# Logits of the second attention branch: two heads on the two halves of the array's rows

## The chip, the core and the metric

The kernel runs on one core of a Trainium2 chip. The metric is the device time of one execution in microseconds (us), the median of several runs. TensorE (PE below) multiplies matrices: it holds a tile of weights in its array, whose rows are the partitions that are summed over, and streams the other operand through; results go to banks of PSUM. VectorE (DVE), ScalarE (ACT) and GpSimd (POOL) work element by element, and SyncE (SP) issues loads. Each engine works through its own queue in order.

## What is computed

One decoder block over 512 tokens of width 1024, all in float32. The normalised input is projected once into the parts of two attention branches, "fox" (f) and "moba" (m), of 8 heads of width 64 each, and into two gates. For the second branch, cut to what matters:

```python
q = partial_rope(rms_norm(to_heads(mq, 8), moba_q_g), positions)   # scaled per channel
k = partial_rope(rms_norm(to_heads(mk, 8), moba_k_g), positions)
logits = q @ k.T * 64 ** -0.5          # 256-key blocks; with 512 tokens and top 3 every
logits = where(causal, logits, -inf)   # earlier block is chosen: plain causal attention
y_moba = softmax(logits) @ v * silu(mz)
```

The first branch has the same form, with a forget term added to its logits. Both outputs are projected, gated, added, projected once more and added to the input.

## The kernel before

**Precision.** Products run on float32 values that are rounded for PE (type fp32r). To keep accuracy each operand is split into a rounded part "hi" and a rest "lo" (ACT makes hi, DVE makes lo as the difference), and a product becomes hi*hi + hi*lo + lo*hi. Projections therefore take three matmuls per tile (L303 to L305, L402 to L404, L676 to L678).

**Stages.** The input projections start, then come four attention groups, one for each branch and half of its heads (fa, fb, ma, mb; four heads each, in two pairs), then the gates and the output projection. `attn_group` returns the pieces of one group as functions: `Tr(pr)` prepares a pair of heads, `Aa(h)` makes the logits and softmax of one head, `Bb(h)` transposes the probabilities and multiplies with V, `Yp(pr)` scales and gates a pair's output. The loop at L937 joins the pieces of a group to a list and deals them out between the units of the projections ("fill") with `inter`: in the third group beside mqb, mkb and mvb, in the fourth beside mzb, wf0, wf1 and wf2. The context has a planner switched on (L1036), which fixes the final order of each engine's queue when the program is built; the order of the calls is what it starts from.

**Tr before (L512).** PE transposes q and k of a pair, so that head 0 lies on partitions 0 to 63 and head 1 on 64 to 127 (L516, L518). Then, for each of the two heads (o = 0, 1), a tile QS gets q's hi on the head's own half (`me`, L525, ACT) and q's lo on the other half (`ot`, L526, DVE); a tile KH gets k's hi on its own half (L528, ACT), and a DMA from ACT's queue copies it to the other half (L529); a tile KL gets k's lo on its own half (L530, DVE). The KL tiles are shared with the first branch, whose forget term lies on rows of the other half; before the second branch starts, `moba_begin` (L492) clears these rows on POOL (L496).

**Aa before (L543).** For each head and each of four rows i of 128 queries, n = 128 * (i + 1) keys are needed. Two products over 128 rows go to one bank of the tag `lg` (two banks): QS * KH gives hi*hi + lo*hi, and QS * KL gives hi*lo, with zeros under the lo half:

```python
T.matmul(lg[:, :n], qs[:, qt], kh[:, :n], start=True, stop=False)     # L552
T.matmul(lg[:, :n], q2[:, qt], kl[:, :n], start=False, stop=True)     # L553
```

DVE adds the mask, scales and takes the row minimum (L555, reading the bank), and ACT takes the exponential and the row sum (L557). After two heads DVE inverts the sums (`inverse_sums`, L572); `sums_out` writes them to memory by way of a transpose (L577) and `sums_in` loads them back spread over partitions (L587, ACT's queue), for POOL's product at L658 and DVE's at L659.

**Other lines that are named.** L421 and L422 are ACT's and DVE's parts of the gate of the second branch (mzb), which empty a bank of the tag `pj`; L603 and L604 split the transposed probabilities; L607 and L608 multiply them with V; L632 and L633 take the two halves of that result.

Of the kernel before, what the change touches and what calls it, by code (L numbers as in the profile page):

```python
# [13 lines left out]
P = 128  # L14
# [15 lines left out]
def fox_moba_kernel(ctx: ExitStack, tc, xT, x, w_in, w_fl, w_fox, w_moba, w_out, cst, rope, out):  # L30
# [22 lines left out]
    def pst(tag, bufs, name):  # L53
        return ps.tile([P, 512], F32, name=name, tag=tag, bufs=bufs)
# [434 lines left out]
            T.transpose(pl[:64, t * P:(t + 1) * P], c4[:, t, :], ident)  # L489
        A.activation(LR, pl[:64, :], AF.Copy)  # L490

    def moba_begin():  # L492
        for o in range(2):
            rows = slice(HD, HD + 32) if o == 0 else slice(0, 32)
            for tl in KLt[o]:
                G.memset(tl[rows, :].bitcast(F32), 0.0)  # L496


    Y = {}
    mkn = con.tile([P, 16, 4], F32, name="negm")  # L500
# [4 lines left out]
    def attn_group(br, half, gq, gk):  # L505
# [6 lines left out]
        def Tr(pr):  # L512
            def go():
                pq, pk = tp("p_qT"), tp("p_kT")
                for t in range(NT):
                    T.transpose(pq[:, t * P:(t + 1) * P], qn[:, t, pr * P:(pr + 1) * P], ident)  # L516
                for t in range(NT):
                    T.transpose(pk[:, t * P:(t + 1) * P], kn[:, t, pr * P:(pr + 1) * P], ident)  # L518
                for o in range(2):
                    h = 2 * pr + o  # L520
                    me, ot = (slice(0, HD), slice(HD, P)) if o == 0 else (slice(HD, P), slice(0, HD))
                    qs = t2("qs", 4, "QS", dt=F32R)
                    kh = t2("qs", 4, "KH", dt=F32R)
                    kl = KLt[o][pr]
                    A.activation(qs[me, :], pq[me, :], AF.Copy, scale=gq[me, :])  # L525
                    V.scalar_tensor_tensor(qs[ot, :], pq[me, :], gq[me, :], qs[me, :].bitcast(F32),  # L526
                                           op0=OP.mult, op1=OP.subtract)
                    A.activation(kh[me, :], pk[me, :], AF.Copy, scale=gk[me, :])  # L528
                    nc.scalar.dma_start(out=kh[ot, :].bitcast(F32), in_=kh[me, :].bitcast(F32))  # L529
                    V.scalar_tensor_tensor(kl[me, :], pk[me, :], gk[me, :], kh[me, :].bitcast(F32),  # L530
                                           op0=OP.mult, op1=OP.subtract)
                    q2 = qs
                    if fox:
                        q2 = Q2t[o]
                        lr = slice(HD, HD + 4) if o == 0 else slice(0, 4)
                        hh = hb + h
                        nc.sync.dma_start(out=q2[lr, :].bitcast(F32), in_=LR[hh:32:8, :].bitcast(F32))
                        nc.sync.dma_start(out=kl[lr, :].bitcast(F32), in_=LR[32 + hh:64:8, :].bitcast(F32))
                        nc.scalar.dma_start(out=q2[me, :].bitcast(F32), in_=qs[me, :].bitcast(F32))
                    st[h] = (qs, kh, kl, q2)  # L540
            return go

        def Aa(h):  # L543
            def go():
                qs, kh, kl, q2 = st[h]
                hh = hb + h
                pts = []
                for i in range(NT):
                    n = P * (i + 1)
                    lg = pst("lg", 2, "lg")  # L550
                    qt = slice(i * P, (i + 1) * P)
                    T.matmul(lg[:, :n], qs[:, qt], kh[:, :n], start=True, stop=False)  # L552
                    T.matmul(lg[:, :n], q2[:, qt], kl[:, :n], start=False, stop=True)  # L553
                    pt = stage["pool"].tile([P, n], F32, name=f"p{i}", tag=f"p{i}", bufs=2)
                    V.tensor_tensor_reduce(pt, lg[:, :n], mask[:, 512 - n:512], -0.125, 3.0e38,  # L555
                                           op0=OP.add, op1=OP.min, accum_out=mkn[:, hh, i:i + 1])
                    A.activation(pt, pt, AF.Exp, bias=mkn[:, hh, i:i + 1], scale=-1.0,  # L557
                                 accum_out=rs[:, hh, i:i + 1])
                    pts.append(pt)
                st[h] = pts  # L560
                if h % 2:
                    inverse_sums(h // 2)
                elif h:
                    sums_in(0)
            return go

# [15 lines left out]
        def sums_in(pr):  # L582
            if last and pr:
                return
            rb = st["r", pr] = stage["pool"].tile([P, S], F32, name="rinv_bc", tag="rinv_bc", bufs=1)
            for o in range(2):
                A.dma_start(out=rb[o * HD:(o + 1) * HD, :],  # L587
                            in_=R_dram[hb + 2 * pr + o].rearrange("t p -> (t p)").partition_broadcast(HD))

        def Bb(h):  # L590
            def go():
                pts, vt = st[h], VT[f"{br}v{half}"]
                o = h % 2
                pv = pst("pv", 1, "pv")

                def blk(dst, i, j):
                    T.transpose(dst, pts[i][:, j * P:(j + 1) * P], ident)

                def spl(p, n):
                    tag, w, bufs = ("pt", 512, 4) if n == 512 else ("pc", 256, 2)  # L600
                    hi = t2(tag, bufs, "pth", (P, w), F32R)
                    lo = t2(tag, bufs, "ptl", (P, w), F32R)
                    A.activation(hi[:, :n], p[:, :n], AF.Copy)  # L603
                    V.tensor_tensor(out=lo[:, :n], in0=p[:, :n], in1=hi[:, :n].bitcast(F32), op=OP.subtract)  # L604
                    return hi, lo
                def pvm(j, hl, c0, n, start, stop):
                    T.matmul(pv[:, P * j:P * j + n], vt[:, j, h, :], hl[0][:, c0:c0 + n], start=start, stop=False)  # L607
                    T.matmul(pv[:, P * j:P * j + n], vt[:, j, h, :], hl[1][:, c0:c0 + n], start=False, stop=stop)  # L608
                pa = tp("p_a")
                for i in range(4):  # L610
                    blk(pa[:, i * P:(i + 1) * P], i, 0)
                pb = tp("p_b")
                for i in range(1, 4):
                    blk(pb[:, (i - 1) * P:i * P], i, 1)
                blk(pb[:, 384:512], 3, 3)
                ha = spl(pa, 512)
                hbb = spl(pb, 512)
                pc = tp("p_cc")
                for i in range(2, 4):
                    blk(pc[:, (i - 2) * P:(i - 1) * P], i, 2)  # L620
# [11 lines left out]
                A.activation(sh[me, :], pv[ot, :], AF.Copy)  # L632
                V.tensor_tensor(out=y[me, :], in0=pv[me, :], in1=sh[me, :], op=OP.add)  # L633
# [29 lines left out]
            return go  # L663


        return ([Tr(0)], [Aa(0), Aa(1), Tr(1), Bb(0), Aa(2), Bb(1), Yp(0), Aa(3)], [Bb(2), Bb(3)], [Yp(1)])


# [268 lines left out]
    for n in range(4):  # L937
        nxt = []

        def following(n=n, nxt=nxt):  # L940
            br, half, cq, ck = plan[n + 1][:4]
            if n == 1:
                moba_begin()
            nxt.extend(attn_group(br, half, col(cq), col(ck)))
            nxt[0][0]()
        fill = filler(plan[n][4])
        if n == 0:
            for k in range(4):
# [91 lines left out]
```

## Time and profile before

| what | value |
|---|---|
| median of three runs | 434.72 us (434.6 to 434.87) |
| the profiled execution, its own time | 434.93 us |
| its span, first to last instruction | 433.2 us |
| granted TensorE clock, mean | 0.999 |
| logits and softmax of the second branch | from 176.9 to 270.7 us of the span |

A profile is one execution. "Busy" on PE is a model: a product lasts longer than the step to the next one, since products overlap. Rows of a timeline give start, duration, engine, line, operation, out<-in, the weight tile (rows*columns) and the moving operand (partitions x columns); in square brackets stands idle time ahead of it and what ended it. Rows of a line or tile give the least, median and greatest duration in ns and when the first and last started. Rows of waits give total us, times and the longest. A window's row gives its length, then busy us and count of PE, PE's weight loads, DVE, ACT and POOL, the granted clock, and the DMA engines' share and GB/s.

### The profile page before, as it was taken

What the parts mean: (1) busy time and instruction counts of PE and PEld (TensorE: products, weight loads), DVE (VectorE), ACT (ScalarE), POOL (GpSimd) and SP (SyncE); (2) the same over time, 40 slices, a digit from 0 to 9 for tenths busy, and PEclk for the clock granted to TensorE, in tenths of its full rate; (3) what the DMA queues carried; (4) which work ended last, traced back from release to release, by engine and by line L of the source; (5) the groups of instructions that cost most, each with busy time, mean ns of one, the idle gap of its engine ahead of it and who ended that gap; (6) DMA issues with size and microseconds to landing.
All of it is one profiled execution on the core that took longest, in us unless ns stands there. A gap on an engine that the chain in (4) does not pass through costs nothing.

```text
span 433.2 us, 8085 instructions
## 1 busy us (share of the span) xinstructions
PE 424.3 (98%) x3103; PEld 400.4 (92%) x3103; DVE 314.0 (72%) x559; ACT 249.4 (58%) x480; POOL 87.4 (20%) x108
## 2 busy tenths in 40 slices
PE   7999989999999999999999999999999999999996
PEld 6998889999999998999998878899999989999996
DVE  5669986677998868767866898959897796674311
ACT  4986335776877866767765855647655545521100
POOL 1049201021433950045630103020000000000000
PEclk9999999999999999999999999999999999999999
DMA  7981266344374424303304304553415306635321
GB/s 249 394 281 61 85 207 196 77 126 126 80 223 163 105 69 123 121 2 123 111 25 134 110 12 160 205 151 96 143 52 193 99 2 213 188 96 160 94 91 38
DMA packets 25671, 56.13 MB, mean 130 GB/s; under 512 B 3240, under 2 KB 11872, under 8 KB 25632
## 3 DMA queue, kind: packets, MB, share of 16 engines
q1 hardware_dynamic: 14528, 40.08, 29.2%
q10 hardware_dynamic: 9952, 11.34, 9.1%
q0 software_dynamic: 1152, 4.19, 2.7%
q8 instruction: 24, 0.39, 0.4%
q14 instruction: 15, 0.12, 0.1%
HBM read 46.01 MB, written 6.32 MB: 121 GB/s over the span
## 4 chain that ended last, share of the span: by engine, by line
PE 83%; DVE 7%; DMA 6%; issue 1%; ACT 1%; SPq 0%; DVEq 0%; ACTq 0%
DMA x<-in_x_dram 3%; PE pb_GA L750 3%; PE pb_GB L747 3%; PE pb_GA L749 3%; PE pb_GA L747 3%; PE pb_GB L750 3%; PE pb_GB L749 3%; PE po L847 3%; PE po L849 3%; PE po L848 3%; DMA xt<-in_xT_dram 3%; PE pv L608 2%; PE pv L607 2%; PE lg L553 2%; PE lg L552 2%; PE pm L676 2%
## 5 line engine op out<-in xcount | busy, mean ns | idle before, releaser
L557 ACT ACTIVATE p<-p,negm 128x128 f32<-128x128 f32 (+1 forms) x64 | 35.7, 558 | 19.2 <-DVE negm L555 18.0
L331 POOL TENSOR_TENSOR ff<-ss,mh 128x8 f32<-128x8 f32 x16 | 27.6, 1733 | 66.6 <-DVE ss L329 43.7
L555 DVE CUSTOM_DVE_ANT_0 p<-lg,mask 128x128 f32<-128x128 f32 (+1 forms) x64 | 30.5, 484 | 11.8 <-PE lg L553 11.3
L847 PE MATMUL po<-wh_wo,mgh 128*128 128x256 f32 x96 | 27.1, 282 | 0.0
L849 PE MATMUL po<-wh_wo,mgl 128*128 128x256 f32 x96 | 27.1, 282 | 0.0
L848 PE MATMUL po<-wl_wo,mgh 128*128 128x256 f32 x96 | 27.0, 281 | 0.0
L857 DVE TENSOR_TENSOR ot<-po,xr 128x256 f32<-128x256 f32 x16 | 6.6, 423 | 24.8 <-PE po L849 23.6
L633 DVE TENSOR_TENSOR ypair<-pv,ysh 64x512 f32<-64x512 f32 x16 | 11.0, 687 | 14.5 <-ACT ysh L632 14.4
L134 ACT ACTIVATE wh_wo<-wr_wo 128x1024 fp32r<-128x1024 f32 x8 | 8.5, 1061 | 21.7 <-PE po L849 8.1
L136 DVE TENSOR_TENSOR wl_GA<-wr_ga,wh_GA 128x1024 fp32r<-128x1024 f32 x14 | 17.9, 1299 | 3.7 <-PE pb_GA L750 2.9
L552 PE MATMUL lg<-KH,QS 128*128 128x128 f32 (+1 forms) x64 | 20.6, 329 | 0.0
L136 DVE TENSOR_TENSOR wl_GB<-wr_gb,wh_GB 128x1024 fp32r<-128x1024 f32 x14 | 16.8, 1222 | 4.2 <-ACT wh_GB L134 3.3
L134 ACT ACTIVATE wh_GA<-wr_ga 128x1024 fp32r<-128x1024 f32 x14 | 14.6, 1058 | 8.6 <-PE pb_GA L749 4.3
L134 ACT ACTIVATE wh_GB<-wr_gb 128x1024 fp32r<-128x1024 f32 x14 | 14.6, 1059 | 8.6 <-PE pm L677 2.5
L848 PEld LDWEIGHTS po<-wl_wo,mgh 128*128 128x128 f32 x96 | 18.1, 189 | 0.0
L847 PEld LDWEIGHTS po<-wh_wo,mgh 128*128 128x128 f32 x96 | 18.1, 189 | 0.0
L849 PEld LDWEIGHTS po<-wh_wo,mgl 128*128 128x128 f32 x96 | 18.1, 189 | 0.0
L136 DVE TENSOR_TENSOR wl_wo<-wr_wo,wh_wo 128x1024 fp32r<-128x1024 f32 x8 | 9.8, 1222 | 7.4 <-ACT wh_wo L134 7.4
L632 ACT ACTIVATE ysh<-pv 64x512 f32<-64x512 f32 x16 | 9.5, 593 | 9.6 <-PE pv L608 8.2
L526 DVE SCALAR_TENSOR_TENSOR QS<-p_qT,cs,QS 64x512 fp32r<-64x512 f32 x16 | 12.0, 750 | 2.6 <-ACT QS L525 2.3
L676 PE MATMUL pf<-yhf,wh_wf 128*128 128x512 f32 x32 | 13.3, 415 | 0.6 <-DVE zs_mzb L422 0.6
L747 PE MATMUL pb_GB<-Gh,wh_GB 128*128 128x256 f32 x48 | 13.5, 281 | 0.0
(447 smaller groups left out, 1768.4 us busy)
## 6 DMA issues: line engine op xcount, KB each, us to landing
wr_ga<-in_w_in_dram SPq DMA_DIRECT2D x8, 512.0 KB
wr_gb<-in_w_in_dram SPq DMA_DIRECT2D x8, 512.0 KB
wr_wo<-in_w_out_dram SPq DMA_DIRECT2D x8, 512.0 KB
xt<-in_xT_dram SPq DMA_DIRECT2D x8, 256.0 KB
x<-in_x_dram SPq DMA_DIRECT2D x8, 256.0 KB
s_dramh<-sum_sh ACTq DMA_DIRECT2D x8, 256.0 KB
s_draml<-sum_sl ACTq DMA_DIRECT2D x8, 256.0 KB
KH<-KH ACTq DMA_DIRECT2D x16, 128.0 KB
```

What stands on the lines that cost most here:

```text
L134: A.activation(hi[:, :, 0:n], src, AF.Copy)
L136: eng.tensor_tensor(out=lo[:, q, 0:n], in0=src[:, q], in1=hi[:, q, 0:n].bitcast(F32), op=OP.subtract)
L331: G.tensor_tensor(out=f2, in0=ss.rearrange("p t h -> p (t h)"), in1=mh, op=OP.pow)
L552: T.matmul(lg[:, :n], qs[:, qt], kh[:, :n], start=True, stop=False)
L555: V.tensor_tensor_reduce(pt, lg[:, :n], mask[:, 512 - n:512], -0.125, 3.0e38, op0=OP.add, op1=OP.min, accum_out=mkn[:, hh, i:i + 1])
L557: A.activation(pt, pt, AF.Exp, bias=mkn[:, hh, i:i + 1], scale=-1.0, accum_out=rs[:, hh, i:i + 1])
L747: T.matmul(o, hi[:, k, cc], lh, start=(n < 3 and c == 0 and k == 0), stop=False, skip_group_check=True)
L749: T.matmul(o, hi[:, k, cc], ll, start=False, stop=False, skip_group_check=True)
L750: T.matmul(o, lo[:, k, cc], lh, start=False, stop=(k == 3), skip_group_check=True)
L847: T.matmul(p[:, :CW], gh[:, st], hi[:, k, :CW], start=(kk == 0), stop=False)
L848: T.matmul(p[:, :CW], gh[:, st], lo[:, k, :CW], start=False, stop=False)
L849: T.matmul(p[:, :CW], gl[:, st], hi[:, k, :CW], start=False, stop=(kk == KT - 1))
```

## The change

In the second branch a pair of heads is prepared as a whole: qh, ql, kh and kl hold both heads, one on each half of the 128 partitions, so that Tr takes two operations of ACT and two of DVE over 128 partitions and no copy. `Am(pr, rows)` takes the place of two `Aa`: for each row it takes both `lg` banks and issues six products over 64 rows, hi*hi, hi*lo and lo*hi, head 0 on the lower half of the array's rows into one bank and head 1 on the upper half into the other, in turn. The softmax part moves to a function `probs` that both branches use. The order of the pieces in a group of the second branch is new, and `moba_begin` is gone.

```diff
-    def moba_begin():
-        for o in range(2):
-            rows = slice(HD, HD + 32) if o == 0 else slice(0, 32)
-            for tl in KLt[o]:
-                G.memset(tl[rows, :].bitcast(F32), 0.0)
...
@@ in Tr, after the transposes
+                if not fox:
+                    qh, kh = t2("qs", 4, "QH", dt=F32R), t2("qs", 4, "KH", dt=F32R)
+                    ql, kl = KLt[0][pr], KLt[1][pr]
+                    for hi, lo, p, g in ((qh, ql, pq, gq), (kh, kl, pk, gk)):
+                        A.activation(hi, p, AF.Copy, scale=g)
+                        V.scalar_tensor_tensor(lo, p, g, hi.bitcast(F32), op0=OP.mult, op1=OP.subtract)
+                    st["qk", pr] = qh, ql, kh, kl
+                    return
...
+        def probs(h, i, lg):
+            n, hh = P * (i + 1), hb + h
+            pt = stage["pool"].tile([P, n], F32, name=f"p{i}", tag=f"p{i}", bufs=2)
+            V.tensor_tensor_reduce(pt, lg[:, :n], mask[:, 512 - n:512], -0.125, 3.0e38,
+                                   op0=OP.add, op1=OP.min, accum_out=mkn[:, hh, i:i + 1])
+            A.activation(pt, pt, AF.Exp, bias=mkn[:, hh, i:i + 1], scale=-1.0,
+                         accum_out=rs[:, hh, i:i + 1])
+            st.setdefault(h, []).append(pt)
...
+        def Am(pr, rows):
+            def go():
+                qh, ql, kh, kl = st["qk", pr]
+                for i in rows:
+                    n = P * (i + 1)
+                    lgs = [pst("lg", 2, "lg") for _ in range(2)]
+                    qt = slice(i * P, (i + 1) * P)
+                    for k, (q, kk) in enumerate(((qh, kh), (qh, kl), (ql, kh))):
+                        for o in range(2):
+                            me = slice(o * HD, (o + 1) * HD)
+                            T.matmul(lgs[o][:, :n], q[me, qt], kk[me, :n], start=(k == 0), stop=(k == 2))
+                    for o in range(2):
+                        probs(2 * pr + o, i, lgs[o])
+                if rows[-1] == NT - 1:
+                    inverse_sums(pr)
+                if pr and not rows[0]:
                     sums_in(0)
+            return go
...
+        if not fox:
+            return ([Tr(0)], [Am(0, (0, 1, 2)), Am(0, (3,)), Tr(1), Bb(0), Bb(1), Am(1, (0, 1, 2)), Yp(0), Am(1, (3,))],
+                    [Bb(2), Bb(3)], [Yp(1)])
         return ([Tr(0)], [Aa(0), Aa(1), Tr(1), Bb(0), Aa(2), Bb(1), Yp(0), Aa(3)], [Bb(2), Bb(3)], [Yp(1)])
...
-            if n == 1:
-                moba_begin()
```

More of the change, by code (lines that the diff above doesn't have):

```diff
@@ L531, in go @@
                                            op0=OP.mult, op1=OP.subtract)
[L532 to L539, printed above, removed]
+                    q2 = Q2t[o]
+                    lr = slice(HD, HD + 4) if o == 0 else slice(0, 4)
+                    hh = hb + h
+                    nc.sync.dma_start(out=q2[lr, :].bitcast(F32), in_=LR[hh:32:8, :].bitcast(F32))
+                    nc.sync.dma_start(out=kl[lr, :].bitcast(F32), in_=LR[32 + hh:64:8, :].bitcast(F32))
+                    nc.scalar.dma_start(out=q2[me, :].bitcast(F32), in_=qs[me, :].bitcast(F32))
                     st[h] = (qs, kh, kl, q2)
             return go
+        def probs(h, i, lg):
[6 more added lines that the diff above has]
+            st.setdefault(h, []).append(pt)
         def Aa(h):
             def go():
-                qs, kh, kl, q2 = st[h]
-                hh = hb + h
-                pts = []
+                qs, kh, kl, q2 = st.pop(h)
                 for i in range(NT):
@@ L553, in go @@
                     T.matmul(lg[:, :n], q2[:, qt], kl[:, :n], start=False, stop=True)
[L554 to L560, printed above, removed]
+                    probs(h, i, lg)
                 if h % 2:
@@ L563, in go @@
                 elif h:
+                    sums_in(0)
+            return go
[15 more added lines that the diff above has]
+                if pr and not rows[0]:
                     sums_in(0)
```

## The prediction

> **What bounds the kernel now.** I read the page's head first (span, busy time, granted clock), then the waits of TensorE (PE), then the windows around the second branch, then the PE timeline there.
>
> ```profile
> span 433.2 us, 8085 instructions
> ...
> PE 424.3 (98%) x3103; PEld 400.4 (92%) x3103; DVE 314.0 (72%) x559; ACT 249.4 (58%) x480; POOL 87.4 (20%) x108
> ...
> PEclk9999999999999999999999999999999999999999
> ```
>
> ```profile
> PE pj_fva L303 <- DVE v_fva L341: 1.5, 1, 1.5
> PE pf L676 <- DVE zs_mzb L422: 0.6, 2, 0.4
> PE p_b L597 <- DVE ptl L604: 0.2, 1, 0.2
> ```
>
> ```profile
> 195.00:200.00 5.00, 5.00 (x45) 5.00 (x44) 4.72 (x6) 4.40 (x8) 1.69 (x3) 1.00 0.58 167
> ...
> 245.00:250.00 5.00, 4.50 (x21) 3.29 (x19) 4.90 (x11) 4.97 (x13) 0.00 (x0) 1.00 0.46 131
> 250.00:255.00 5.00, 4.70 (x22) 3.74 (x23) 4.87 (x12) 3.28 (x8) 0.00 (x0) 1.00 0.12 26
> 255.00:260.00 5.00, 5.00 (x29) 4.19 (x28) 4.97 (x9) 1.99 (x7) 0.00 (x0) 1.00 0.00 1
> ```
>
> PE is busy for 424.3 of 433.2 us, at full granted clock in every slice. In the part that changes (its logits run from 176.9 us, in a row below, and its last products to about 282) its only recorded waits are the 0.6 and 0.2 us above, in the two windows in which it is below 5.00; there DVE, and in the first of them ACT, are as good as full. (The 1.5 us lie ahead of this part.) So two things can move the end: how long the logit products occupy PE, and those 0.8 us. Busy time can't be used for the first, since products overlap. What counts is the step from one start to the next, and one head of the second branch shows every size:
>
> ```profile
> 186.35 0.22 PE L552 MATMUL lg<-KH,QS 128*128 128x128 f32 x1
> 186.41 0.27 PE L553 MATMUL lg<-KL,QS 128*128 128x128 f32 x1
> 186.52 0.33 PE L552 MATMUL lg<-KH,QS 128*128 128x256 f32 x1
> 186.69 0.28 PE L553 MATMUL lg<-KL,QS 128*128 128x256 f32 x1
> 186.81 0.34 PE L608 MATMUL pv<-ptl,v_fvb 128*128 128x384 f32 x1
> ...
> 189.19 0.34 PE L552 MATMUL lg<-KH,QS 128*128 128x384 f32 x1
> 189.38 0.34 PE L553 MATMUL lg<-KL,QS 128*128 128x384 f32 x1
> 189.55 0.28 PE L303 MATMUL pj_mqb<-wh_mqb,Gh 128*128 128x256 f32 x1
> ...
> 189.78 0.40 PE L552 MATMUL lg<-KH,QS 128*128 128x512 f32 x1
> 190.02 0.39 PE L553 MATMUL lg<-KL,QS 128*128 128x512 f32 x1
> 190.25 0.28 PE L305 MATMUL pj_mqb<-wh_mqb,Gl 128*128 128x256 f32 x1
> ```
>
> ```profile
> L553 PE MATMUL lg<-KL,QS x32: 221/332/397, 176.9 to 267.4; 128*128 128x128 f32 x8, 128*128 128x256 f32 x8, 128*128 128x384 f32 x8, 128*128 128x512 f32 x8
> ```
>
> The two rows of 128 and 256 columns take 186.81 - 186.35 = 0.46 us for four products, 0.115 each; 384 columns take 0.36 / 2 = 0.18; 512 take 0.47 / 2 = 0.235. Width sets the step from 256 columns up (0.235 is twice 0.115); 128 columns cost as much as 256, so there something else is the floor, most likely the load of the next weights, for which the trace has a row in the next part. One head costs 0.46 + 0.36 + 0.47 = 1.29 us, and the eight heads 10.3 us. That is the sum that the change edits; the row of L553 shows that the 32 rows of the eight heads have these four widths, eight times each.
>
> **The change part by part.** *The products.* Before, a head's row takes two products over 128 rows (L552, L553; the second multiplies zeros with half of its rows). After, a row of a pair takes six over 64 rows, three on each half of the array, the halves in turn: 4 pairs x 4 rows x 6 = 96 products in place of 64. No row of this trace has a product of 64 rows, so its step is bounded from both sides. If the two halves run side by side, two products take one step, and a pair costs three steps per row: 3 x (0.115 + 0.115 + 0.18 + 0.235) = 1.94 us, four pairs 7.7, which is 2.6 us less. If they follow one another, each takes a full step: 15.5 us, 5.2 more. Between lie the weights:
>
> ```profile
> L552 PEld LDWEIGHTS lg<-KH,QS x64: 187/188/193, 79.1 to 267.0; 128*128 128x128 f32 x64
> ```
>
> Each product has its own load, 188 ns long and overlapped to a floor of 0.115 us per product. If the products pair but the loads of both halves still queue, two products take at least 0.23 us: a pair costs 3 x (0.23 + 0.23 + 0.23 + 0.235) = 2.78 us, four pairs 11.1, which is 0.8 us more than now. I take the first value, loads and products side by side, because the halves share neither rows nor banks nor weights; the ends are -2.6 and +5.2. The Trainium skill (TensorE: Matmul & The Clock Gate, Part 3, The mechanism) says that products on different row groups start about 4 ns apart and that loads overlap where the row groups differ; by it the sum is the first value. No run here shows it yet.
>
> *Going from whole array to halves and back.* Each of the 16 rows of pairs is a block of its own among products of 128 rows: 32 changes. The nearest row is a product whose weights are 8 columns wide, amid 128-wide ones:
>
> ```profile
> 96.94 0.28 PE L305 MATMUL pj_fvb<-wh_fvb,Gl 128*128 128x256 f32 x1
> 97.06 0.27 PE L577 MATMUL p_ri<-ident,rinv 128*8 128x128 f32 x1
> 97.08 0.36 PE L303 MATMUL pj_fvb<-wh_fvb,Gh 128*128 128x256 f32 x1
> 97.29 0.28 PE L304 MATMUL pj_fvb<-wl_fvb,Gh 128*128 128x256 f32 x1
> ```
>
> Three products in 97.29 - 96.94 = 0.35 us are 0.117 each, the ordinary step. So going to a narrower weight tile and back costs nothing that can be seen, and I take nothing for the halves too. The upper bound: a product lasts 0.39 us at a step of 0.235, so a tail of 0.16 us is normally overlapped; if the next kind had to wait for it, 32 x 0.16 = 5.1 us; if its load (188 ns) could not run ahead either, 32 x 0.35 = 11.2 us. The Trainium skill (TensorEngine Tiling (Array Packing), Tiling Modes, Key Properties) speaks against this change: "Changing tiling mode (not just tile) drains the TensorE". The four rows above do not show such a drain for narrower columns; for halves of the rows no run here shows it. By that rule the gain is gone; it is a rival below.
>
> *The preparation (Tr).* Before, a pair takes four ACT and four DVE operations over 64 partitions and two DMAs that copy KH to the other half:
>
> ```profile
> L525 ACT ACTIVATE QS<-p_qT,cs x16: 669/682/686, 74.0 to 249.4; 64x512 fp32r<-64x512 f32 x16
> L528 ACT ACTIVATE KH<-p_kT,cs x16: 668/676/687, 74.6 to 249.9; 64x512 fp32r<-64x512 f32 x16
> L526 DVE SCALAR_TENSOR_TENSOR QS<-p_qT,cs,QS x16: 743/751/757, 74.7 to 252.0; 64x512 fp32r<-64x512 f32 x16
> L530 DVE SCALAR_TENSOR_TENSOR KL<-p_kT,cs,KH x16: 734/750/757, 75.5 to 253.3; 64x512 fp32r<-64x512 f32 x16
> L529 ACTq DMA_DIRECT2D KH<-KH x16: 467/484/688, 75.4 to 250.8; - x16
> L633 DVE TENSOR_TENSOR ypair<-pv,ysh 64x512 f32<-64x512 f32 x16 | 11.0, 687 | 14.5 <-ACT ysh L632 14.4
> L604 DVE TENSOR_TENSOR ptl<-p_a,pth x16: 672/688/692, 90.2 to 278.6; 128x512 fp32r<-128x512 f32 x16
> ```
>
> L633 over 64 partitions and L604 over 128 both take 0.69 us, so half the operations do the same work: per pair 2 x 0.68 us of ACT, 2 x 0.75 of DVE and 2 x 0.48 of issue go; over four pairs 5.4, 6.0 and 3.9 us. Nearly all of it is hidden under PE. It counts only where PE waits:
>
> ```profile
> 247.79 0.75 DVE L526 SCALAR_TENSOR_TENSOR QS<-p_qT,cs,QS 64x512 fp32r<-64x512 f32 x1
> 248.57 0.74 DVE L530 SCALAR_TENSOR_TENSOR KL<-p_kT,cs,KH 64x512 fp32r<-64x512 f32 x1
> ...
> 250.44 0.67 DVE L422 SCALAR_TENSOR_TENSOR zs_mzb<-sg,pz_mzb 128x512 f32<-128x512 f32 x1
> ```
>
> Two splits of 0.75 us stand in DVE's queue ahead of the gate (L422) for whose bank PE waits; one such pair less would let it through 1.5 us sooner. At most the 0.8 us come back, at least nothing, since another operation can take that place; I take 0.5. The four clears on POOL (moba_begin, L496) fall away on an engine that is busy for 20% of the span: nothing.
>
> *The order.* The softmax operations (L555, L557) stay 64 each, at the same sizes. A row now takes both `lg` banks at once, and the next row of a pair needs both read. The reads are two L555 per row:
>
> ```profile
> L555 DVE CUSTOM_DVE_ANT_0 p<-lg,mask x64: 236/481/692, 79.6 to 269.3; 128x128 f32<-128x128 f32 x16, 128x256 f32<-128x256 f32 x16, 128x384 f32<-128x384 f32 x16, 128x512 f32<-128x512 f32 x16
> ```
>
> That is about 1 us of DVE per row before PE may write the next one. Behind a waiting product everything on PE queues. The cover is the other work of PE: of the 106 us of this part only 10.3 are logits, so some 6 us of projections, transposes and value products fall to each of the 16 blocks. I cost it at nothing; without cover it would be 12 rows (those that follow one of their own pair) x 1 us = 12 us. The reload of the inverse sums (L587) is now issued from ACT's queue behind Bb(1), nearer to its reader on POOL (L658) and, through that, to DVE's L659. In the last group that reader stood so:
>
> ```profile
> L658 POOL TENSOR_TENSOR rinv_bc<-zs_mzb,rinv_bc x1: 1295/1295/1295, 263.3 to 263.3; 128x512 f32<-128x512 f32 x1
> ```
>
> ```profile
> 274.50 0.68 DVE L659 TENSOR_TENSOR ypair<-ypair,rinv_bc 128x512 f32<-128x512 f32 x1
> ```
>
> POOL's product ended 10 us before DVE took it up, so there is slack: nothing.
>
> **Sum.** The profiled execution took 434.93 us (span 433.2, and 1.7 outside it), 0.2 above the median 434.72. Products -2.6, waits -0.5, all else nothing: -3.1, so 431.8 from this execution and 431.6 from the median; I say 431.7.
>
> **The rivals.**
> 1. *The loads queue* although the products pair: +0.8 - 0.5 = +0.3, so 435.0, within measurement. For it: the floor of 0.115 us at 128 columns shows loads one behind the other on the whole array. Against it: those use the same rows. Chance 0.18.
> 2. *Each change between whole array and halves drains* (slower): 32 x 0.16 = +5.1 - 3.1 = +2.0, so 436.8, and up to 443 with loads that can't run ahead. It decides from 3.1 / 32 = 0.10 us per change on. For it: the tail of 0.16 us exists and must go somewhere when the array is divided; the planner may also put a product of another unit between the six, which adds changes. Against it: the 0.117 us steps around L577. Chance 0.20; of this about a fifth with so small a drain that a gain over 0.2% is left.
> 3. *The halves run one after the other*, so the change doesn't do what it says: +5.2 - 0.5, so 439.4. For it: no product in this trace shares the array. Against it: different rows, different banks. Chance 0.15.
> 4. *The two banks hold PE up*: a quarter of the 12 uncovered follow-on rows lose 1 us each, +3, which brings 434.7; it decides where less than 1 us of other PE work lies between two rows. Before, no wait of PE on an `lg` bank is recorded, but then the rows took turns. Chance 0.09.
>
> **How the numbers follow.** My forecast has 0.38, the rivals 0.18, 0.20, 0.15 and 0.09. A measurement of this kernel can tell about 0.2% (0.9 us) from no change. Faster: 0.38 + 0.04 of rival 2 = 0.42. Same: most of rivals 1 and 4, less what spills over, 0.18. Slower: 0.40 from rivals 2 and 3 and the spill of 1 and 4. The range reaches down to 430.8 (0.8 us of waits regained and a little less of the floor) and up to 438.0, which holds rivals 1 and 4, and rival 2 up to 0.2 us per change; out of it stay rival 3 and the worst of 2. The forecast's own range is 430.8 to 433.
>
> **What would show it.** In the changed kernel's timeline the six products of a row should start in twos, almost together; the step from the first product of a block of 384 or 512 columns to whatever follows the block should be 3 x 0.18 or 3 x 0.235 us. 128- and 256-column blocks of 0.69 us in place of 0.35 mean rival 1; blocks of twice the length at 512 columns mean rival 3; correct block lengths with 0.1 to 0.35 us lost before the first and behind the last product mean rival 2; recorded waits of PE on L555 mean rival 4. ACT and DVE should lose 5 to 6 us of busy time each. The forecast is wrong if the time between 176 and 282 us doesn't shrink by some 3 us.

## The result, and the profile after

The changed kernel takes 446.48 us (median of four runs, 446.31 to 447.09) against 434.66 us for the kernel before on the same chip (434.6 to 434.87). The ratio is 1.0276, with a 95% interval of 1.026 to 1.0291: slower by about 12 us. The forecast was 431.7, with a range up to 438.0.

The head of the page of the kernel after:

```profile
span 445.4 us, 8090 instructions
...
PE 436.2 (98%) x3135; PEld 401.5 (90%) x3135; DVE 306.2 (69%) x551; ACT 243.8 (55%) x472; POOL 83.5 (19%) x104
...
PEclk9999999999999999999999999999999999999999
```

The span grew by 12.2 us, at the same granted clock. DVE lost 7.8 us of work and ACT 5.6, as the smaller `Tr` should give. PE has 32 products more and is as full as before, so busy shares don't say where the time went. The waits of PE don't either (all that are recorded; total us, times, longest):

```profile
PE pv L628 <- DVE ypair L654: 1.6, 1, 1.6
PE warm_ps L107 <- DVE fg_pre L468: 1.5, 1, 1.5
PE pj_fva L303 <- DVE v_fva L341: 1.3, 1, 1.3
PE fqa L379 <- ACT Zh L125: 0.3, 1, 0.3
```

The 0.6 us behind the gate are gone as forecast, a wait of 1.6 us in the tail of the last group is new, and no row names a logit bank. What the page offers is first and last starts of the units, which date the loss. After:

```profile
L303 PE MATMUL pj_mva<-wh_mva,Gh x32: 276/280/367, 145.1 to 163.1; 128*128 128x256 f32 x32
...
L303 PE MATMUL pj_mvb<-wh_mvb,Gh x32: 275/281/381, 216.4 to 232.6; 128*128 128x256 f32 x32
```

and before:

```profile
L303 PE MATMUL pj_mva<-wh_mva,Gh x32: 276/280/367, 144.8 to 162.8; 128*128 128x256 f32 x32
...
L303 PE MATMUL pj_mvb<-wh_mvb,Gh x32: 278/281/366, 212.1 to 226.8; 128*128 128x256 f32 x32
```

Up to the second branch the two kernels are 0.3 us apart (163.1 and 162.8). At the end of mvb, the unit beside which the first of its two groups has run, they are 5.8 us apart (232.6 and 226.8), and no wait of PE is recorded in between. About half of the loss thus falls into each group.

**One block, step by step.** The PE timeline of the kernel after around the 256-column row of the first pair ("x2" is two products that are shown as one row since they run together):

```profile
182.70 0.28 PE L304 MATMUL pj_mqb<-wl_mqb,Gh 128*128 128x256 f32 x1
182.82 0.39 PE L628 MATMUL pv<-pth,v_fvb 128*128 128x512 f32 x1
183.13 0.39 PE L579 MATMUL lg<-KH,QH 64*128 64x256 f32 x2
183.36 0.28 PE L579 MATMUL lg<-KL,QH 64*128 64x256 f32 x2
183.48 0.28 PE L579 MATMUL lg<-KH,KL 64*128 64x256 f32 x2
183.69 0.38 PE L305 MATMUL pj_mqb<-wh_mqb,Gl 128*128 128x256 f32 x1
183.91 0.28 PE L303 MATMUL pj_mqb<-wh_mqb,Gh 128*128 128x256 f32 x1
```

and PE's weight loads there:

```profile
183.13 0.19 PEld L579 LDWEIGHTS lg<-KH,QH 64*128 64x128 f32 x2 [0.24 <-issue]
183.24 0.19 PEld L579 LDWEIGHTS lg<-KL,QH 64*128 64x128 f32 x2
183.36 0.19 PEld L579 LDWEIGHTS lg<-KH,KL 64*128 64x128 f32 x2
183.68 0.19 PEld L305 LDWEIGHTS pj_mqb<-wh_mqb,Gl 128*128 128x128 f32 x1
183.79 0.19 PEld L303 LDWEIGHTS pj_mqb<-wh_mqb,Gh 128*128 128x128 f32 x1
```

Read the differences of the starts. L628 with 512 columns should step by about 0.23 us and takes 0.31: 0.08 lost ahead of the block. The first pair should step by 0.12 and takes 0.23, because its load starts only with it (183.13) and not 0.1 us ahead as in a dense row: 0.11 lost. The second pair steps by 0.12, as a single product of this width does, so the halves and their loads do run side by side. The third takes 0.21: 0.09 lost ahead of the change back. Then the first product over the whole array, whose load again starts with it (183.68), takes 0.22: 0.10 lost. Each change thus costs some 0.09 us ahead of it and 0.10 us behind it: 0.19, and the block 0.39. That the load doesn't run ahead holds for all 54 changes of this trace: there the load starts 1 to 3 ns ahead of its product, elsewhere 115 ns (the median). That the 0.09 us are the array running empty is a reading; no row shows it.

**Not all products are in pairs.** Two blocks of one 512-column row, with seven projections between them (five left out here):

```profile
190.16 0.28 PE L303 MATMUL pj_mqb<-wh_mqb,Gh 128*128 128x256 f32 x1
190.37 0.49 PE L579 MATMUL lg<-KH,QH 64*128 64x512 f32 x1
190.70 0.39 PE L579 MATMUL lg<-KL,QH 64*128 64x512 f32 x1
190.93 0.39 PE L579 MATMUL lg<-KH,KL 64*128 64x512 f32 x1
191.25 0.39 PE L304 MATMUL pj_mqb<-wl_mqb,Gh 128*128 128x256 f32 x1
...
192.07 0.28 PE L304 MATMUL pj_mqb<-wl_mqb,Gh 128*128 128x256 f32 x1
192.28 0.49 PE L579 MATMUL lg<-KH,QH 64*128 64x512 f32 x1
192.62 0.39 PE L579 MATMUL lg<-KL,QH 64*128 64x512 f32 x1
192.85 0.39 PE L579 MATMUL lg<-KH,KL 64*128 64x512 f32 x1
```

Here "x1" says that the two heads went one after the other, 1.9 us apart: the order that the planner fixed sends one head's three products when the first bank is free and the other's later. That row costs six steps and four changes. Counted over the whole PE timeline, the 96 products of 64 rows stand in 27 blocks (not 16): 28 pairs and 40 singles. Of the 16 rows, six are whole, six have their heads apart like this one (12 blocks), and four are cut by one or two whole products in between (9 blocks).

**The sum.** Over all PE rows of a trace I add the steps from start to start. What a step would take in a dense row is 0.112 us or, if that is more, 0.4475 ns per column plus 3 ns (this gives 0.118, 0.175 and 0.232 us for 256, 384 and 512 columns, as the dense rows show). The rest I divide into what stands at the edges of blocks of 64 rows (their own steps, and those just ahead of and behind them), and all else ("waits": recorded ones, start-up, small gaps). Later tables use the same columns, in us:

| kernel | span | logit steps at full rate | blocks | cost of the edges | waits and the rest |
|---|---|---|---|---|---|
| before | 433.2 | 10.18 | 0 | 0 | 8.10 |
| after | 445.4 | 11.53 | 27 | 10.07 (0.373 each) | 8.84 |

1.35 + 10.07 + 0.74 = 12.2 us, which is the difference of the spans. The mean of a block is a little under 0.39 us because two steps serve two blocks at once, where a single whole product stands between them, and because some 128-column products behind a block lose only 0.05 us.

### The profile page after: what moved, and what is told of

Same layout as the page of the kernel before. It is cut to its first block, busy times and chain, and to the rows that moved or that the text cites. A ratio compares the mean times of both kernels' runs of the same rounds, so it can differ in the third digit from the quotient of the medians.

```text
span 445.4 us, 8090 instructions
## 1 busy us (share of the span) xinstructions
PE 436.2 (98%) x3135; PEld 401.5 (90%) x3135; DVE 306.2 (69%) x551; ACT 243.8 (55%) x472; POOL 83.5 (19%) x104
## 4 chain that ended last, share of the span: by engine, by line
PE 84%; DVE 6%; DMA 6%; ACT 1%; issue 1%; SPq 0%; DVEq 0%; ACTq 0%
PE lg L579 4%; DMA x<-in_x_dram 3%; PE pb_GB L771 3%; PE pb_GB L774 3%; PE pb_GB L773 3%; PE pb_GA L771 3%; PE pb_GA L774 3%; PE pb_GA L773 3%; PE po L871 3%; PE po L873 3%; PE po L872 3%; DMA xt<-in_xT_dram 3%; PE pv L628 2%; PE pv L629 2%; PE pf L701 2%; PE pf L700 2%
## 5 line engine op out<-in xcount | busy, mean ns | idle before, releaser
L549 ACT ACTIVATE p<-p,negm 128x128 f32<-128x128 f32 (+3 forms) x64 | 35.8, 560 | 26.2 <-DVE negm L547 25.4
L547 DVE CUSTOM_DVE_ANT_0 p<-lg,mask 128x128 f32<-128x128 f32 (+3 forms) x64 | 30.4, 486 | 14.2 <-PE lg L579 8.3
L136 DVE TENSOR_TENSOR wl_GA<-wr_ga,wh_GA 128x1024 fp32r<-128x1024 f32 x14 | 16.9, 1222 | 5.0 <-PE pb_GA L774 4.3
L625 DVE TENSOR_TENSOR ptl<-p_a,pth 128x512 fp32r<-128x512 f32 x16 | 11.0, 686 | 4.4 <-ACT pth L624 4.3
L771 PE MATMUL pb_GA<-Gh,wh_GA 128*128 128x256 f32 x48 | 13.6, 283 | 0.0
L773 PE MATMUL pb_GA<-Gl,wh_GA 128*128 128x256 f32 x48 | 13.6, 283 | 0.0
```

The costliest lines, as they stand in the source:

```text
L136: eng.tensor_tensor(out=lo[:, q, 0:n], in0=src[:, q], in1=hi[:, q, 0:n].bitcast(F32), op=OP.subtract)
L771: T.matmul(o, hi[:, k, cc], lh, start=(n < 3 and c == 0 and k == 0), stop=False, skip_group_check=True)
L773: T.matmul(o, hi[:, k, cc], ll, start=False, stop=False, skip_group_check=True)
```

## Experiments

My theory after the result: the changes between the whole array and half of its rows cost 0.19 us each, and the singles lose the gain of the products. The rivals: the new order with both banks taken together costs the time (through waits that the profile books elsewhere); the six smaller products are dear in themselves; or any narrower tile, of rows or columns, is.

### The order and both banks, without halves

`whole_new_order` is the kernel before with `Am` and the new list of pieces, but with the old L552 and L553 over 128 rows:

```diff
+                    for o in range(2):
+                        qs, kh, kl, q2 = st[2 * pr + o]
+                        T.matmul(lgs[o][:, :n], qs[:, qt], kh[:, :n], start=True, stop=False)
+                        T.matmul(lgs[o][:, :n], q2[:, qt], kl[:, :n], start=False, stop=True)
...
+            return ([Tr(0)], [Am(0, (0, 1, 2)), Am(0, (3,)), Tr(1), Bb(0), Bb(1), Am(1, (0, 1, 2)), Yp(0), Am(1, (3,))],
```

> The kernel before with its own preparation and its whole-array products, but with the new order of pieces and both lg banks taken by one row of a pair. Theory (each change between products of 128 and of 64 rows costs about 0.19 us, so 0.39 us a block, and nothing else matters): no such change is left, so within 1 us of before, 434 to 436 us. Rival (the two banks and the new order hold TensorE up): it keeps most of the 11.8 us and comes out at 443 to 447.

Measured: 439.71 us against 434.55, ratio 1.0118 (1.01 to 1.0136). There is no product of half the rows in it, and it still loses 5 us; its steps at full rate are those of before. That lies between the two ranges: "changes alone" falls as a theory, and the rival is right that the order has a price of its own, though not most of the loss.

`whole_three` is the kernel after with its products over all 128 rows, so that each row of a pair takes six whole products (both banks then hold the sum of two heads, so only its time is of use):

```diff
-                            T.matmul(lgs[o][:, :n], q[me, qt], kk[me, :n], start=(k == 0), stop=(k == 2))
+                            T.matmul(lgs[o][:, :n], q[:, qt], kk[:, :n], start=(k == 0), stop=(k == 2))
```

> The changed kernel with each of its 96 products over all 128 rows (which sums the two heads of a pair into both banks, so the logits are not the reference's). Theory: no change of mode is left; 96 full steps in place of 64 cost 15.3 in place of 10.2 us, +5.1, and some 0.4 us of other waits: 439 to 441, faster than the changed kernel although nothing runs side by side. Rival (three products per head, the two banks and the order are the cost): as the changed kernel, 446 to 448, or 5 us more.

Measured: 440.47 us against 434.55, ratio 1.0133 (1.0116 to 1.015), within the theory's range. Its source differs from the kernel after by the slices of this one line, though the planner orders it anew. Its timeline at the row that was split above:

```profile
189.49 0.28 PE L303 MATMUL pj_mqb<-wh_mqb,Gh 128*128 128x256 f32 x1
189.61 0.40 PE L579 MATMUL lg<-KH,QH 128*128 128x512 f32 x1
189.84 0.40 PE L579 MATMUL lg<-KL,QH 128*128 128x512 f32 x1
190.08 0.39 PE L579 MATMUL lg<-KH,KL 128*128 128x512 f32 x1
190.31 0.28 PE L304 MATMUL pj_mqb<-wl_mqb,Gh 128*128 128x256 f32 x1
```

The edges are gone: 0.12 us from L303 to the first logit product, 0.23 behind the last. The same products on half of the rows, some of them in pairs, take 3.74 us less at full rate and 10.07 us of edges: 3.74 less and 10.07 more are 6.3; with 0.3 more of waits that is the 6.6 by which the spans differ (445.4 and 438.8).

| kernel | span | logit steps at full rate | blocks | cost of the edges | waits and the rest |
|---|---|---|---|---|---|
| whole_new_order | 437.8 | 10.18 | 0 | 0 | 12.72 |
| whole_three | 438.8 | 15.27 | 0 | 0 | 8.55 |

`whole_three` has 5.09 us more of products than before, but only 0.45 us more of waits, where `whole_new_order` has 4.6 more. The two share the order and the banks, but not the preparation (`whole_three` has no copies of KH) nor the length of PE's work. So the waits of the order are not a constant that adds up; whether the copies or PE's later arrival makes the difference is not separated by these two. Nor is it all waiting. Of the 4.2 us between them, 2.6 lie between 240 and 260 us and 1.4 between 280 and 300 us. There both wait for `ypair`, 1.7 and 1.6 us, but only in `whole_new_order` does the granted clock then fall (0.86 in this window; 1.00 in `whole_three`):

```profile
280.00:290.00 10.00, 8.30 (x55) 7.83 (x55) 6.11 (x11) 5.57 (x11) 3.31 (x5) 0.86 1.01 369
```

Why it falls in one and not in the other stays open.

`order_alone` is the kernel before with only Bb(1) and Aa(2) exchanged in the list of the second branch:

```diff
+        if not fox:
+            return ([Tr(0)], [Aa(0), Aa(1), Tr(1), Bb(0), Bb(1), Aa(2), Yp(0), Aa(3)], [Bb(2), Bb(3)], [Yp(1)])
```

> The kernel before with nothing changed but the order of the pieces in the second branch: Bb(1) ahead of Aa(2), as the pair products need it. Whole-array products, one head at a time, one lg bank a row. Theory (what whole_new_order lost is the order: the second pair's softmax comes after both value products of the first, and TensorE runs short of work at the end of the stage): 437 to 440 us. Rival (it lost by taking two banks at once): 434.3 to 435.5.

Measured: 436.67 us against 434.91, ratio 1.0048 (1.0027 to 1.0069), between the two ranges. The waits of PE show where:

```profile
PE lg L552 <- DMA KH<-KH: 2.0, 1, 2.0
```

Here the first logits of a pair wait 2.0 us for the copy of KH, which the kernel after doesn't have. So this exchange costs 1.8 us in the old kernel, by a wait that belongs to the old preparation; it can't be carried over as a term of the new one.

### All pairs together

`halves_together` is the kernel after with the logit products at high priority for the planner, and with the first of each row waiting until both banks have been read:

```diff
+                            with tc.high_priority():
+                                mm = T.matmul(lgs[o][:, :n], q[me, qt], kk[me, :n], start=(k == 0), stop=(k == 2))
+                            if k == 0 and o == 0:
+                                tc.add_manual_dep(mm.ins, READS[-1].ins.name, mybir.DependencyInfo(
+                                    mybir.DependencyClass.Sync, mybir.DependencyReason.DATA), reason="both banks")
```

> The changed kernel with the six products of a row kept together (high priority, and the first waits until both banks are read): 19 blocks in the planned order in place of 27, all 96 products in pairs. Theory: 19 x 0.39 = 7.4 us of changes, 7.7 us of products in place of 10.2: +4.9 on before, 439 to 440.5 us. Rival (banks): the first product now waits for the later of both banks, so as slow as the changed kernel or slower, 446 to 450.

Measured: 445.0 us against 434.55, ratio 1.0239 (1.0219 to 1.0259): between theory and rival again. All 96 products are now in 48 pairs, and the blocks fall to 19. Products and edges do what the theory says (the table below), but the time doesn't follow. Its waits of PE:

```profile
PE p_a L624 <- ACT p L551: 2.4, 1, 2.4
...
PE pv L634 <- DVE ypair L660: 1.4, 1, 1.4
...
PE pv L634 <- ACT pth L630: 0.5, 1, 0.5
```

and the window in which the 2.4 us fall:

```profile
280.00:290.00 10.00, 6.91 (x37) 5.34 (x37) 5.70 (x12) 5.04 (x12) 1.81 (x4) 0.83 0.72 255
```

PE stands idle in the tail of the last group, waiting for the softmax of the last row, and there the granted clock was 0.83 (the next column after the five engines). How the edit brings this about (most likely the earlier logits leave less other work to lie under the tail) was not tested by itself.

### Fewer blocks

`halves_fewer_blocks` adds to this that rows 2 and 0 of a pair share a bank (384 and 128 columns) and one block:

```diff
+                for grp in rows:
+                    at = dict(zip(grp, (0, 384)))
...
+                                    mm = T.matmul(lgs[o][:, c:c + n], q[me, i * P:i * P + P], kk[me, :n],
+                                                  start=(k == 0 and i == grp[0]), stop=(k == 2), skip_group_check=True)
...
+            return ([Tr(0)], [Am(0, ((2, 0), (1,))), Am(0, ((3,),)), Tr(1), Bb(0), Bb(1), Am(1, ((2, 0), (1,))), Yp(0), Am(1, ((3,),))],
```

> As halves_together, and rows 2 and 0 of a pair share the two banks, so that their twelve products are one block: 15 blocks in the planned order. Theory: 15 x 0.39 = 5.9 us of changes, 7.7 us of products: +3.4 on before, 437.5 to 439 us, about 1.5 below halves_together. Rival (banks): no faster than halves_together, since the banks are held longer.

Measured: 440.52 us against 434.55, ratio 1.0145 (1.0119 to 1.0171); 15 blocks. It is 4.5 us below `halves_together`, where 1.5 was expected, and still 1.5 above the range; its edges are 1.4 us less, the rest is waits and the clock, which stayed at 1.00 here. `halves_twelve_blocks` lets the first product of a block also wait for the pair's last rest part, so that nothing can come between:

```diff
+                        st["lo", pr] = V.scalar_tensor_tensor(lo, p, g, hi.bitcast(F32), op0=OP.mult, op1=OP.subtract)
...
+                                    for w in (READS[-1], st["lo", pr]):
+                                        tc.add_manual_dep(mm.ins, w.ins.name, mybir.DependencyInfo(
+                                            mybir.DependencyClass.Sync, mybir.DependencyReason.DATA), reason="both banks")
```

> As halves_fewer_blocks, and the first product also waits until both lo parts of the pair are ready, so that no block is cut: 12 blocks in place of 15. If TensorE's own work sets the time: 3 x 0.36 = 1.1 us less than halves_fewer_blocks, 439 to 439.7. If the softmax chain at the end of the stage sets it, as the waits of that kernel near 281 to 287 us suggest: no faster, 440 to 441.

Measured: 437.51 us against 434.91, ratio 1.0062 (1.0045 to 1.008); 12 blocks. This is better than either range: 1.2 us less of edges than `halves_fewer_blocks`, and 1.7 us less of waits, which no expectation had. A 512-column row of it:

```profile
187.16 0.28 PE L304 MATMUL pj_mqb<-wl_mqb,Gh 128*128 128x256 f32 x1
187.37 0.50 PE L583 MATMUL lg<-KH,QH 64*128 64x512 f32 x2
187.71 0.39 PE L583 MATMUL lg<-KL,QH 64*128 64x512 f32 x2
187.94 0.40 PE L583 MATMUL lg<-KH,KL 64*128 64x512 f32 x2
188.26 0.39 PE L305 MATMUL pj_mqb<-wh_mqb,Gl 128*128 128x256 f32 x1
```

Three steps for two heads (0.34, 0.23, 0.32 with the edges in them), where the kernel after took twice as many. The three variants in one table:

| kernel | span | logit steps at full rate | blocks | cost of the edges | waits and the rest |
|---|---|---|---|---|---|
| halves_together | 442.9 | 7.64 | 19 | 6.79 (0.357 each) | 13.55 |
| halves_fewer_blocks | 438.2 | 7.64 | 15 | 5.35 (0.357) | 10.24 |
| halves_twelve_blocks | 435.3 | 7.64 | 12 | 4.14 (0.345) | 8.57 |

The mean price of a block holds at 0.345 to 0.373 us over four kernels, so the number of blocks times it is a sound term. The last column is not forecast by it: `halves_together` and `halves_fewer_blocks` came out slower than by products and edges alone, by 5.4 and 2.1 us of waits in the tail, which in `halves_together` include the steps at the lower clock. `halves_twelve_blocks` has only 0.5 us more of them than before, and its -2.54 + 4.14 + 0.47 = 2.1 us is the difference of its span. It is the best version with halves that ran, and it doesn't beat the kernel before.

### The change of rows by itself

Four kernels leave the second branch alone and alter one product of the output projection, the last third of `po` (L849 before), where PE is dense and nothing else is near.

`out_half_rows_single` takes every such product (96) over 64 rows, each between two whole ones:

```diff
-                    T.matmul(p[:, :CW], gl[:, st], hi[:, k, :CW], start=False, stop=(kk == KT - 1))
+                    T.matmul(p[:, :CW], gl[:HD, st], hi[:HD, k, :CW], start=False, stop=(kk == KT - 1))
```

> The kernel before; in the output projection (columns 1 to 3 of four, 12 units of 24 products) every third product, the one with the merged values' lo part, takes only the lower 64 rows, which leaves half of that correction out. 96 products of 64 rows, each alone between products of 128 rows: 192 changes, nothing else moved, no bank or order touched. Theory: 96 x 0.39 = +37 us, 470 to 474. Rival (a change costs nothing; the loss lies in the attention stage): no change, 434 to 435.

`out_half_rows_grouped` has the same products, moved into a loop of their own at the end of each output tile, eight in a row (12 blocks; the last ends PE's work, so that 11 have a change back and are counted below):

```diff
+            for hf in range(2):
+                hi, lo = chunks[f"wo{n}"][hf]
+                for k in range(4):
+                    kk = 4 * hf + k
+                    gh, gl = MG[kk]
+                    T.matmul(p[:, :CW], gl[:HD, st], hi[:HD, k, :CW], start=False, stop=(kk == KT - 1))
```

> The same 96 products of 64 rows, but the eight of a unit stand together at its end: 12 blocks, 24 changes. Theory: 12 x 0.39 = +4.7 us, 438.5 to 440.5. If products of 64 rows were slow in themselves, as slow as out_half_rows_single; if nothing costs, 434 to 435.

`out_half_columns_single` halves the columns of the weight tile (the output channels) in place of its rows, but for the last product of a tile:

```diff
+                    c = P if kk == KT - 1 else HD
+                    T.matmul(p[:c, :CW], gl[:, t * P:t * P + c], hi[:, k, :CW], start=False, stop=(kk == KT - 1))
```

> The same place, but 84 products (seven of the eight of a unit) take a weight tile of 128 rows and 64 columns in place of 128, which leaves that correction out for half of the rows of the output tile. Each stands alone. If only a change of the rows costs, as the eight-column product of the prediction suggested: 434 to 435. If any change of the array's division costs the same: 84 x 0.39 = +33 us, 466 to 469.

`out_half_rows_sparse` takes 64 rows in every fourth of these products only, 24 in all:

```diff
+                    c = HD if k == 1 else P
+                    T.matmul(p[:, :CW], gl[:c, st], hi[:c, k, :CW], start=False, stop=(kk == KT - 1))
```

> As out_half_rows_single, but only 24 of the products take 64 rows, one among twelve, each alone: 48 changes. In out_half_rows_single the granted clock fell to half in this stage, so its price per change is not one at full clock. Theory: at one block in some 1.7 us the clock stays full and a block costs 0.39 us: +9.4 us, 443.5 to 445. If the price grows with the clock's fall here too: 447 to 455.

Measured:

| kernel | us | before, same chip | ratio (95%) | blocks | cost per block |
|---|---|---|---|---|---|
| out_half_rows_single | 514.49 | 435.0 | 1.183 (1.1795 to 1.1864) | 96 | 0.83 |
| out_half_rows_grouped | 439.28 | 435.0 | 1.01 (1.0071 to 1.013) | 11 | 0.40 |
| out_half_columns_single | 434.45 | 435.0 | 0.999 (0.9978 to 1.0002) | 0 | 0 |
| out_half_rows_sparse | 444.3 | 434.91 | 1.0215 (1.0194 to 1.0235) | 24 | 0.39 |

The timeline of `out_half_rows_sparse` around one such product:

```profile
401.13 0.28 PE L848 MATMUL po<-wl_wo,mgh 128*128 128x256 f32 x1
401.34 0.38 PE L850 MATMUL po<-wh_wo,mgl 64*128 64x256 f32 x1
401.65 0.39 PE L847 MATMUL po<-wh_wo,mgh 128*128 128x256 f32 x1
401.87 0.28 PE L848 MATMUL po<-wl_wo,mgh 128*128 128x256 f32 x1
401.99 0.28 PE L850 MATMUL po<-wh_wo,mgl 128*128 128x256 f32 x1
```

The steps are 0.21, 0.31 and 0.22 where the dense step is 0.12: 0.09, 0.19 and 0.10 lost, as in the kernel after. In `out_half_columns_single`, tiles of half the columns follow whole ones without any loss:

```profile
400.86 0.28 PE L848 MATMUL po<-wl_wo,mgh 128*128 128x256 f32 x1
400.97 0.28 PE L850 MATMUL po<-wh_wo,mgl 128*64 128x256 f32 x1
401.09 0.28 PE L847 MATMUL po<-wh_wo,mgh 128*128 128x256 f32 x1
```

So it is the halving of the rows, with no second half beside it, no bank, no softmax and no order in play. It is paid per change and not per product (eight in a row cost what one costs). Three of the four came out within the ranges that go with such a price for rows alone; `out_half_rows_single` came out at 514 us where 470 to 474 was expected. The windows of that stage say why:

```profile
380.00:400.00 20.00, 20.00 (x128) 17.21 (x127) 9.97 (x15) 4.81 (x6) 0.00 (x0) 1.00 0.34 111
400.00:420.00 20.00, 20.00 (x52) 12.75 (x52) 2.24 (x4) 0.00 (x0) 0.00 (x0) 0.53 0.09 27
420.00:440.00 20.00, 20.00 (x50) 12.69 (x49) 3.47 (x5) 2.12 (x2) 0.00 (x0) 0.50 0.08 26
```

From about 401 us on the granted clock is half, while PE's busy time reads 20.00 of 20. This kernel's 0.83 us therefore mixes two things and isn't used for the price: by the same reckoning its first eight blocks, at full clock, cost 0.39 us each, and those at half clock 0.88.

## Why the prediction was wrong

**The step that failed** is the second term, "going from whole array to halves and back": "I take nothing for the halves too". It was sized from a product with 8 weight columns amid wider ones, and `out_half_columns_single` shows that a narrower tile is indeed free, while a shorter one (64 rows) is not: 0.19 us per change. Columns were no neighbour of rows, though they were the nearest row of the trace. This is rival 2, whose two ends, 0.16 and 0.35 us, hold the value; its point of decision, 0.10 us per change, was passed by a factor of two. The rule that the prediction quoted from the Trainium skill (TensorEngine Tiling (Array Packing), Tiling Modes, Key Properties), that a change of tiling mode drains the array, agrees with the kernel after and with `out_half_rows_sparse` for rows; for columns the trace of `out_half_columns_single` shows no drain.

**Its second part** is the count. The prediction took 32 changes, one block for each row of a pair, and noted only in rival 2 that the planner might cut blocks. There were 54. The sum from the forecast to the result, in terms of spans (433.2 - 3.1 = 430.1 forecast, 445.4 measured, 15.3 apart):

- the 32 changes at 0.186 us instead of 0: +6.0
- 22 further changes, 12 since six rows had their heads sent apart and 10 since whole products cut four others: +4.1
- 40 products alone instead of in pairs: 11.53 instead of 7.64, +3.9
- waits: +0.74 instead of -0.5, +1.2

That is 15.2 us; the last 0.1 is rounding (2.6 was taken for the pairs, 2.54 is counted). With the price right and the count as assumed, the prediction would have been 437.7. That is still inside the stated range, which took in a change of up to 0.2 us; what carries the result out of it is the count and the products sent alone, 8.0 us.

**The products** were right. The prediction took loads and products of the two halves side by side, 7.7 us for all four pairs, 2.6 less. Where all products are in pairs they take 7.64, 2.54 less than 10.18. Rival 1 (loads queue) and rival 3 (halves serial) are out: pairs appear as "x2", with the two starts mostly 3 or 4 ns apart and at most 17, and a pair's step is that of one product. The rule of the Trainium skill (TensorE: Matmul & The Clock Gate, Part 3, The mechanism) that products on different row groups start about 4 ns apart and that their loads overlap agrees.

**The preparation** was right in size: 5.6 us of ACT and 7.8 of DVE are gone (5.4 and 6.0 in the working; DVE's other 1.8 aren't the operations of `Tr`), under PE's cover. The wait for the gate's bank (0.6) went as said, but 1.6 us came late elsewhere, at `pv` L628 behind DVE's `ypair` in the tail: the prediction had named that risk ("another operation can take that place") and still counted half a microsecond as won.

**The order** was costed at nothing. In the kernel after this is nearly what is seen (+0.74 us of waits and rest), but the cover is thinner than the prediction had it: `whole_new_order` has 4.6 us more of waits than before and `halves_together` 5.4, the lower clock of their tails included. That the kernel after escapes them because its slower blocks bring PE late enough for the softmax to be ready fits `whole_three`, but is argued and not shown. Rival 4, waits on the banks, isn't recorded as waits of PE; the two banks acted when the program was ordered, by parting the heads of a row. That this is what parts them rests on `halves_together`, in which the wait for both banks (with the priority) makes all of them pairs; the two edits weren't tried apart.

**Could a better order pay?** By the steps measured here, a block of one row saves one step of four, at most 0.235 us (512 columns), and costs 0.34 to 0.39, in no case under 0.26: it loses at every width. All products together save 2.54 us, so no more than seven blocks could break even, two rows or more in each. Twelve is what two banks gave here. Fewer would need more banks at a time, and a different place for the probabilities, whose tiles (two of each width) a pair takes up whole, which forces Bb(1) ahead of the next pair. Neither was tried, and the waits of the tail would have to stay hidden besides.

## What to carry to other kernels

Count the changes between the whole array and part of its rows before counting what the packing saves: at 0.19 us each way, a block of packed products must save more than 0.39 us, which a block of three steps instead of four doesn't do at 512 columns or fewer. When a cost has no row in the trace, ask whether the nearest row shares the mechanism (columns and rows did not), and let the break-even price, here 0.10 us, say how much trust that row must bear. And where a planner orders the instructions, products that should run together have to be tied together, and a saving on the busiest engine may come back as a wait in the tail.

## What the runs showed of the hardware that was not expected

- A change between weight tiles of 128 and of 64 rows costs 0.19 us in either direction at full granted clock (`out_half_rows_sparse`, the kernel after): 0.09 ahead of the change, and 0.10 behind it, where the load starts with its product and not 0.115 us ahead. Tiles of 64 columns (`out_half_columns_single`) or 8 (the kernel before) among tiles of 128 cost nothing.
- With every third product on 64 rows (`out_half_rows_single`) the granted clock fell, some 6 us into the stage, to 0.53 and then 0.50 for the rest of it, though the busy share of PE read full; with every twelfth (`out_half_rows_sparse`) the mean clock stayed at 1.0. Where between these it turns was not tried.
